# Output projection of a hybrid decoder trunk in three passes instead of two, with new hand-over times

## The chip, the core and the metric

One core of a Trainium2 chip runs the whole program. Its engines each have their own instruction queue and take it strictly in order: TensorE (PE in the profile, with PEld for its weight loads), VectorE (DVE), ScalarE (ACT), GpSimd (POOL) and SyncE (SP), which here only issues DMAs. They wait for each other by semaphores. The metric is the device time of one execution in microseconds (us); less is better.

## The reference, cut to what matters

```python
for l in range(2):                                   # D=1024, 512 tokens
    p = rms_norm(h, attn_norm[l]) @ w_in[l]          # one projection, three groups of columns
    y_a = rwkv7_mixer(p[:, :896], ...)               # 4 heads of 64: 256 columns
    y_b = retention_mixer(p[:, 896:1920], ...)       # 4 heads of 64: 256 columns
    y_c = mla_mixer(p[:, 1920:], ...)                # latent attention, 8 heads of 64: 512 columns
    h = h + concat(y_a, y_b, y_c) @ w_out[l]         # the output projection
    gu = rms_norm(h, ffn_norm[l]) @ w_gate_up[l]
    h = h + (silu(gu[:, :2816]) * gu[:, 2816:]) @ w_down[l]
return rms_norm(h, final_norm)
```

## The kernel before, in words

Activations lie transposed: 128 channels on the partitions, 512 tokens along the free axis. A float32 operand is split into a rounded part `hi` and a remainder `lo`, and each weight tile into `wh` and `wl` (ACT casts `wh`, L410; DVE or POOL subtracts `wl`, L411), so each product takes three matmuls of 128x128 by 128x512: `wh·hi`, `wh·lo`, `wl·hi` (`gemm`). Weight tiles come from DRAM by SP into three buffers `wr` (`fetch`, L394); the first tiles of the feed-forward's down weights come into the single buffer `gg`, which until then holds the RWKV gate that `group_norm` multiplies with (L890). The tile numbers in `POOL_LO` have their `wl` made on POOL.

`mix[0..7]` are the eight blocks of 128 channels of the concatenated mixers: 0 and 1 from RWKV-7 (`group_norm`), 2 and 3 from retention (`retnet`), 4 to 7 from latent attention (`attend`). An attention head is three score tiles in PSUM (`pd<-u,u`, closed by the causal mask `pd<-cmb,idb`), row maxima (DVE, L983), exponentials (ACT, L985), scaling by 1/sum (L218, parts on DVE and on POOL by `EN` keys `x0` to `x3`), ten transposes (`pm<-ident`, L257), copies (L1000) and, for a pair of heads, `attend` (`pm<-u,u` with 64 columns of weights), whose result L304 and L305 split. Score tiles and dense products share four PSUM banks `pd`.

The output projection (from L1297) waits until `mix[0..3]` are all there, then makes for each of the eight output blocks `m` one PSUM tile of four products (12 matmuls) in the order k = 2, 3, 0, 1, and adds it to the residual `h_` (L1309). The residual is loaded from DRAM just before (L1303). A second part takes `mix[4..7]` in the same way (L1328), its first four blocks without `mix[7]` at first.

The order of all instructions is set at build time by `Driver`. Every mixer, head, group norm and the dense chain is a generator; at each `yield` it hands over. The driver always resumes the ready task of the lowest priority number, keeps a clock that only matmuls advance, and holds a task back for the number of us it yielded, `T[l][key]`. The keys `p_...` are priorities. `dense()` has priority 9, the lowest, so its matmuls fill what the others leave. Engines then run that order; nothing is moved at run time.

Of the kernel before, what the change touches and what calls it, by code (L numbers as in the profile page):

```python
# [23 lines left out]
KT = D // P  # L24
# [108 lines left out]
def lay_out(inp):  # L133
# [56 lines left out]
def tile_trunk(ctx: ExitStack, tc: tile.TileContext, a: dict, out: bass.AP, dbg=None):  # L190
    nc = tc.nc
    act, dve, pool, sp = nc.scalar, nc.vector, nc.gpsimd, nc.sync
# [45 lines left out]
    def psd():  # L238
        return pd.tile([P, S], F32, tag="pd", name=nm("pd"))
# [823 lines left out]
    def dense():  # L1063
        hk = lambda k: h_[k // 2][:, k % 2, :]
# [35 lines left out]
        for l in range(L):  # L1100
            st = {"mix": [None] * KT, "rkv": {}, "qa": [], "ka": [], "PT": {}, "heads": 0}
            mix = st["mix"]
# [7 lines left out]
            ps = psd()  # L1110
# [394 lines left out]
```

## Time and profile before

| | |
|---|---|
| three runs | 1312.43 us median (1306.7 to 1313.23) |
| profiled execution | 1308.13 us, of which 1306.3 us are the profile's span |
| mean granted TensorE clock | 0.993 |
| PE / PEld / DVE / ACT / POOL busy | 1266.3 / 1088.7 / 982.6 / 680.7 / 91.8 us |
| first and last L1309 | 250.9 us and 921.3 us from the span's start |

All stretches below are in us from the span's start. The mixers of layer 0 end near 276 us, those of layer 1 near 925 us; the long runs between are the feed-forward. "Idle" of an engine is span less busy time. Matmuls are pipelined and their ends are modelled, so 24 matmuls in a row take less than 24 times the mean of one.

### The profile page before, as it was taken

The numbers are of one execution on the slowest core, as the hardware profiler recorded it, in microseconds if no ns is written. First come the engines' busy times: TensorE is split into PE (matmuls) and PEld (weight loads), VectorE is DVE, ScalarE is ACT, GpSimd is POOL, SyncE is SP. The second block draws the span as 40 slices with busy tenths as digits, with TensorE's granted clock in tenths as the row PEclk, the third lists the DMA queues.
The fourth block names the chain that finished last, engine by engine and source line by source line (L and its number), as shares of the span: only waits on it lengthen the run. The fifth ranks groups of instructions, "written<-read, shape, count | busy, mean of one in ns | idle before, by whom it ended". The sixth has DMA issues, their size and how long they took to land.

```text
span 1306.3 us, 20183 instructions
## 1 busy us (share of the span) xinstructions
PE 1266.3 (97%) x7802; PEld 1088.7 (83%) x7802; DVE 982.6 (75%) x1653; ACT 680.7 (52%) x1271; POOL 91.8 (7%) x79
## 2 busy tenths in 40 slices
PE   7999999899999999999999998989999999999997
PEld 5788787578899999999877887857788999999996
DVE  7797887747987777777668697585579877777774
ACT  7834456735554444445475345474455544444454
POOL 1040112100000000000012300122100000000000
PEclk9999999999999999999999999989999999999999
DMA  7435421223233333333522523141222333222231
GB/s 243 143 91 158 101 70 46 97 65 97 81 113 98 97 99 111 98 97 106 185 89 85 134 85 77 44 141 41 83 96 67 113 99 112 97 98 97 82 113 65
DMA packets 67512, 131.14 MB, mean 100 GB/s; under 512 B 29044, under 2 KB 33940, under 8 KB 67416
## 3 DMA queue, kind: packets, MB, share of 16 engines
q1 hardware_dynamic: 66040, 128.23, 31.3%
q8 instruction: 61, 1.00, 0.3%
q10 hardware_dynamic: 1232, 1.09, 0.2%
q0 software_dynamic: 144, 0.52, 0.1%
q14 instruction: 35, 0.29, 0.1%
HBM read 117.50 MB, written 9.18 MB: 97 GB/s over the span
## 4 chain that ended last, share of the span: by engine, by line
PE 88%; DVE 6%; ACT 3%; DMA 1%; issue 1%; SPq 0%; DVEq 0%; ACTq 0%
PE pd L250 61%; PE pm L250 25%; PE pm L257 2%; DMA wr<-in_wts_dram 1%; DMA u<-in_xT_dram 1%; DVE wl L411 0%; DVE r L729 0%; DVE r L1467 0%; DVE u L1034 0%; ACT wh L410 0%; DVE r L348 0%; DVE u L1024 0%; DVE u L723 0%; DVE u L719 0%; DVE u L1245 0%
## 5 line engine op out<-in xcount | busy, mean ns | idle before, releaser
L250 PE MATMUL pd<-u,wh 128*128 128x256 f32 (+1 forms) x3136 | 757.1, 334 | 10.7 <-ACT wh L410 5.8
L250 PEld LDWEIGHTS pd<-u,wh 128*128 128x128 f32 x3136 | 529.8, 191 | 73.5 <-issue 8.7
L250 PE MATMUL pd<-u,wl 128*128 128x256 f32 (+1 forms) x1568 | 518.6, 331 | 0.7 <-DVE wl L429 0.6
L250 PEld LDWEIGHTS pd<-u,wl 128*128 128x128 f32 x1568 | 298.7, 191 | 29.4 <-POOL wl L411 0.9
L250 PE MATMUL pm<-u,wh 128*128 128x512 f32 (+1 forms) x800 | 212.0, 352 | 0.7 <-DVE u L1034 0.7
L410 ACT CAST wh<-wr 128x1024 fp32r<-128x1024 f32 (+3 forms) x102 | 98.8, 974 | 148.7 <-PE pd L250 95.8
L250 PEld LDWEIGHTS pm<-u,wh 128*128 128x128 f32 x800 | 139.1, 190 | 18.8 <-DVE u L1034 0.9
L250 PE MATMUL pm<-u,wl 128*128 128x512 f32 (+1 forms) x400 | 140.3, 351 | 0.0
L428 ACT CAST wh<-r 128x512 fp32r<-128x512 f32 x144 | 87.4, 618 | 97.6 <-PE pm L250 51.4
L411 DVE TENSOR_TENSOR wl<-wr,wh 128x1024 fp32r<-128x1024 f32 (+3 forms) x88 | 102.6, 1170 | 41.0 <-ACT wh L410 40.7
L428 ACT CAST wh<-wr 128x512 fp32r<-128x512 f32 x108 | 67.0, 620 | 81.0 <-PE pm L250 54.1
L429 DVE TENSOR_TENSOR wl<-r,wh 128x512 fp32r<-128x512 f32 x144 | 97.6, 687 | 7.6 <-ACT wh L428 5.5
L429 DVE TENSOR_TENSOR wl<-wr,wh 128x512 fp32r<-128x512 f32 x108 | 74.3, 689 | 24.5 <-ACT wh L428 22.3
L250 PEld LDWEIGHTS pm<-u,wl 128*128 128x128 f32 x400 | 75.7, 189 | 10.3
L1390 DVE TENSOR_TENSOR u<-u,pm 128x512 f32<-128x512 f32 x64 | 43.6, 684 | 43.5 <-PE pm L250 43.5
L250 PE MATMUL pm<-u,u 32*32 32x32 f32 (+4 forms) x728 | 67.4, 277 | 4.9 <-DVE u L749 2.8
L411 POOL TENSOR_TENSOR wl<-wr,wh 128x1024 fp32r<-128x1024 f32 (+3 forms) x14 | 29.7, 2125 | 594.1 <-ACT wh L410 594.1
L250 PEld LDWEIGHTS pm<-u,u 32*32 32x32 f32 (+3 forms) x728 | 50.4, 157 | 21.9 <-issue 14.5
L410 ACT CAST wh<-gg 128x1024 fp32r<-128x1024 f32 x32 | 33.6, 1050 | 41.5 <-issue 27.4
L439 DVE TENSOR_TENSOR r<-r,wr 128x512 f32<-128x512 f32 x72 | 49.5, 688 | 0.6
L250 PE MATMUL pd<-u,u 96*128 96x128 f32 (+3 forms) x128 | 45.1, 465 | 4.2 <-ACT u L985 3.4
L411 DVE TENSOR_TENSOR wl<-gg,wh 128x1024 fp32r<-128x1024 f32 x32 | 39.1, 1222 | 7.7 <-ACT wh L410 7.7
(272 smaller groups left out, 1563.8 us busy)
## 6 DMA issues: line engine op xcount, KB each, us to landing
wr<-in_wts_dram SPq DMA_DIRECT2D x142, 512.0 KB, 3.6
gg<-in_wts_dram SPq DMA_DIRECT2D x32, 512.0 KB, 3.3
wr<-in_wts_dram SPq DMA_DIRECT2D x22, 384.0 KB, 3.0
u<-in_xT_dram SPq DMA_DIRECT2D x7, 512.0 KB, 6.3
tb<-tab_d SPq DMA_DIRECT2D x8, 256.0 KB, 4.1
r<-r SPq DMA_DIRECT2D x32, 64.0 KB, 2.0
h_d<-u SPq DMA_DIRECT2D x4, 512.0 KB, 2.7
u<-h_d SPq DMA_DIRECT2D x4, 512.0 KB, 6.5
```

The source lines that it names most:

```text
L250: tc.keep_in_program_order(nc.tensor.matmul(o, lhsT, rhs, start=start, stop=stop, skip_group_check=True))
L257: tc.keep_in_program_order(nc.tensor.transpose(o, x, idn))
L410: act.copy(hi[:, z], t[:, z])
L411: (pool if on in POOL_LO else dve).tensor_tensor(lo[:, z], t[:, z], hi[:, z].bitcast(F32), ALU.subtract)
L428: act.copy(hi[:, z], t)
L429: dve.tensor_tensor(lo[:, z], t, hi[:, z].bitcast(F32), ALU.subtract)
L439: E(key).tensor_tensor(o, x, y, ALU.add)
L1390: dve.tensor_tensor(hk(m), hk(m), ps, ALU.add)
```

## The change

The residual is loaded before the projection's first wait. The first part becomes two passes over all eight output blocks: the first waits only for `mix[2]` and `mix[3]` (retention), the second for `mix[0]` and `mix[1]` (RWKV). Each block then has two products (6 matmuls) per PSUM tile and its own add into the residual, so L1309 runs 32 times instead of 16. The weights are laid out to fit; their bytes and the number of matmuls stay. The third pass, over `mix[4..7]`, is as before.

The tables are set anew. In `EN`, `e563` (a subtraction in RWKV of layer 1) goes from POOL to DVE; `e759` (L890, the gate in `group_norm`), `h1` (the remainder of RWKV's low-rank inputs, L314) and `x0` (the 128-column part of the softmax scaling, L218) go from DVE to POOL. `POOL_LO` has 15 tiles instead of 13. In `T`, most values move; the priorities of layer 0 become 3.43 for RWKV (7.42 before), 6.66 for heads (8.88) and 6.0 for `attend` (0), those of layer 1 become 5.43 for RWKV (0), 7.16 for retention (5.86) and 0 for heads (3.43).

```diff
-POOL_LO = (0, 21, 23, 26, 32, 35, 106, 115, 127, 129, 132, 134, 137)
+POOL_LO = (0, 12, 21, 23, 26, 27, 30, 35, 38, 106, 110, 115, 129, 134, 137)
...
-        for k0 in (0, 512):
-            ws += [np.concatenate([kblk(w, b(P * m), slice(k0, k0 + 512)) for m in (2 * i, 2 * i + 1)], 1) for i in range(4)]
+        for k0 in (256, 0):
+            ws += [np.concatenate([kblk(w, b(P * m), slice(k0, k0 + 256)) for m in range(4 * i, 4 * i + 4)], 1) for i in range(2)]
+        ws += [np.concatenate([kblk(w, b(P * m), slice(512, 1024)) for m in (2 * i, 2 * i + 1)], 1) for i in range(4)]
...
-            yield lambda: all(mix[k] is not None for k in range(4))
-            w = wnext()
             h_ = [ua([P, 2, S]) for _ in range(4)]
             h_src = a["xT"] if l == 0 else h_d
             with tc.issue_after(stream["dma"].ins):
                 for i in range(4):
                     sp.dma_start(h_[i], h_src[:, 2 * i : 2 * i + 2, :])
-            for m in range(KT):
-                if m % 2 == 0 and m > 0:
-                    w = wnext()
-                ps = psd()
-                yield from gemm(ps, w, mix, [(4 * (m % 2) + k, k) for k in (2, 3, 0, 1)])
-                dve.tensor_tensor(hk(m), hk(m), ps, ALU.add)
+
+            for k0 in (2, 0):
+                yield lambda: mix[k0] is not None and mix[k0 + 1] is not None
+                for m in range(KT):
+                    if m % 4 == 0:
+                        w = wnext()
+                    ps = psd()
+                    yield from gemm(ps, w, mix, [(2 * (m % 4) + k, k0 + k) for k in range(2)])
+                    dve.tensor_tensor(hk(m), hk(m), ps, ALU.add)
```

PE in layer 0, where the last steps of the RWKV chains (`Sb`, `R`) meet the first heads. Before, no dense product stands here (nor in the 120 matmuls that follow):

```order
L250 MATMUL pm_2170<-u_644,Sb_312_1693 128x128
L257 MATMUL pm_2177<-ident,r_377_2010 128x128
L257 MATMUL pm_2177<-ident,u_2009 128x128 x3
L250 MATMUL pm_2124<-u_955,u_954 128x128
L250 MATMUL pm_2124<-u_748,u_955 128x128
L250 MATMUL pm_2170<-R_427_2169,u_1436 128x128
L250 MATMUL pm_2191<-u_955,u_748 128x128
```

Of the change, the same place (lines are one higher; `wh_1871` and `wl_1872` are the retention pass's first weights):

```order
L251 MATMUL pm_2170<-u_644,Sb_312_1693 128x128
L251 MATMUL pd_2191<-u_1552,wh_1871 128x512 x2
L251 MATMUL pd_2191<-u_1552,wl_1872 128x512
L258 MATMUL pm_2195<-ident,r_377_2010 128x128
L258 MATMUL pm_2195<-ident,u_2009 128x128 x3
L251 MATMUL pm_2124<-u_955,u_954 128x128
L251 MATMUL pm_2124<-u_748,u_955 128x128
L251 MATMUL pm_2170<-R_427_2169,u_1436 128x128
L251 MATMUL pd_2191<-u_1742,wh_1871 128x512 x2
L251 MATMUL pd_2191<-u_1742,wl_1872 128x512
L251 MATMUL pm_2212<-u_955,u_748 128x128
```

The retention pass is strewn in threes among chains and heads. From here to the layer's last `attend` PE now has 111 matmuls of the projection where it had 84: 27 more.

PE in layer 1, after the scores of heads 0 to 2. Before, three matmuls of a query projection, then the third head's second and third score tile, then transposes:

```order
L250 MATMUL pd_8452<-u_8014,wh_8293 128x512 x2
L250 MATMUL pd_8452<-u_8014,wl_8294 128x512
L250 MATMUL pd_8546<-u_8046,u_8376 128x384
...
L250 MATMUL pd_8558<-cmb,idb 128x256
L257 MATMUL pm_8574<-ident,u_8459 128x128
L257 MATMUL pm_8574<-ident,r_1578_8460 128x128
```

Of the change (`wh_8367` and `wl_8368` are the retention pass):

```order
L251 MATMUL pd_8569<-cmb,idb 128x256
L251 MATMUL pd_8468<-u_8030,wh_8309 128x512 x2
L251 MATMUL pd_8468<-u_8030,wl_8310 128x512
L251 MATMUL pd_8602<-u_7846,wh_8367 128x512 x2
L251 MATMUL pd_8602<-u_7846,wl_8368 128x512
L251 MATMUL pd_8602<-u_7985,wh_8367 128x512 x2
L251 MATMUL pd_8602<-u_7985,wl_8368 128x512
...
L258 MATMUL pm_8627<-ident,u_8475 128x128
L258 MATMUL pm_8627<-ident,r_1586_8476 128x128
```

All nine score tiles of heads 0 to 2 now stand first, then 21 dense matmuls in one block, then the transposes. From there on heads follow each other closely: from the second head's scores to the layer's last `attend` PE has 42 dense matmuls where it had 100: 58 fewer. Everything ahead of this place in layer 1 is in the same order on PE, but for one swap of 3 and 21 matmuls.

SP in layer 0, where RWKV's last parts have gone through DRAM (`ro_d`) and the projection's weights (`wr`) begin. Before, the residual (`u<-in_xT_dram`) stands behind `gg`:

```order
L394 DMA wr_2678<-in_wts_dram 128x1024
L394 DMA wr_2722<-in_wts_dram 128x1024
L394 DMA gg_3215<-in_wts_dram 128x1024
L1303 DMA u_2520<-in_xT_dram 128x1024
L1303 DMA u_2521<-in_xT_dram 128x1024
L1303 DMA u_2522<-in_xT_dram 128x1024
L1303 DMA u_2523<-in_xT_dram 128x1024
L394 DMA wr_2768<-in_wts_dram 128x1024
```

Of the change, the same place on SP, where `wr_2608` is the retention pass's first weights:

```order
L395 DMA wr_2608<-in_wts_dram 128x1024
L395 DMA wr_2724<-in_wts_dram 128x1024
L1302 DMA u_2177<-in_xT_dram 128x1024
L1302 DMA u_2178<-in_xT_dram 128x1024
L1302 DMA u_2179<-in_xT_dram 128x1024
L1302 DMA u_2180<-in_xT_dram 128x1024
L395 DMA wr_2772<-in_wts_dram 128x1024
L395 DMA gg_3231<-in_wts_dram 128x1024
```

The four loads of the residual now go ahead of `gg`. In layer 1 they still stand behind `gg`, but no longer behind the `wr` that followed it.

## Rows read from the trace of the kernel before

**Rows 1.** The page, part 1: busy time (share) x instructions of each engine.

```profile
PE 1266.3 (97%) x7802; PEld 1088.7 (83%) x7802; DVE 982.6 (75%) x1653; ACT 680.7 (52%) x1271; POOL 91.8 (7%) x79
```

**Rows 2.** Busy time by 20 us stretches; columns in the first line.

```profile
core 0: us, PE busy (x) PEld busy (x) DVE busy (x) ACT busy (x) POOL busy (x), PEclk, DMA share, GB/s
220.00:240.00 20.00, 17.33 (x97) 10.76 (x97) 14.06 (x37) 18.07 (x44) 6.24 (x5) 1.00 0.00 1
240.00:260.00 20.00, 18.57 (x108) 13.09 (x105) 15.69 (x39) 13.80 (x34) 2.49 (x2) 1.00 0.45 158
320.00:340.00 20.00, 20.00 (x90) 16.57 (x89) 19.89 (x32) 9.08 (x12) 0.00 (x0) 1.00 0.25 79
880.00:900.00 20.00, 20.00 (x108) 14.23 (x107) 12.34 (x35) 10.46 (x31) 3.73 (x3) 1.00 0.22 80
```

**Rows 3.** The two attention stages, each to the layer's last attend; same columns.

```profile
216.70:275.20 58.50, 54.34 (x303) 37.81 (x301) 38.10 (x90) 37.58 (x91) 8.73 (x7) 1.00 0.22 72
852.60:924.30 71.70, 67.21 (x342) 45.85 (x340) 47.95 (x118) 39.53 (x97) 15.23 (x11) 0.95 0.24 80
```

**Rows 4.** VectorE in time: the last split of retention and of RWKV, layer 0.

```profile
178.45 0.69 DVE L305 TENSOR_TENSOR u<-r,u 128x512 fp32r<-128x512 f32 x1
...
246.50 1.31 DVE L305 TENSOR_TENSOR u<-r,u 128x512 fp32r<-128x512 f32 x2
```

**Rows 5.** TensorE in time, layer 0: instructions that PE waited for.

```profile
234.73 0.44 PE L257 MATMUL pm<-ident,u 128*128 128x128 f32 x2 [1.19 <-ACT r L885]
237.91 0.33 PE L257 MATMUL pm<-ident,u 128*128 128x128 f32 x1 [1.05 <-ACT r L885]
239.69 1.72 PE L250 MATMUL pm<-u,u 128*64 128x512 f32 x8 [0.42 <-DVE r L886]
244.08 0.33 PE L257 MATMUL pm<-ident,u 128*128 128x128 f32 x1 [1.43 <-DVE u L218]
```

**Rows 6.** The chain that ended last: start us, us, what; 36 dense matmuls in a row.

```profile
749.92 8.19 PE pd L250 x36
```

**Rows 7.** TensorE in time, layer 1: score tiles that PE waited for.

```profile
854.83 1.10 PE L250 MATMUL pd<-u,u 96*128 96x512 f32 x2 [0.81 <-PE pd L250]
...
861.07 1.65 PE L250 MATMUL pd<-u,u 96*128 96x384 f32 x2 [3.35 <-ACT u L985]
```

**Rows 8.** The chain that ended last, layer 1: what led to those scores.

```profile
858.11 0.81 ACT r L887
...
858.94 1.28 ACT L985
```

**Rows 9.** Busy time after that wait, layer 1; columns as in rows 2.

```profile
861.00:880.00 19.00, 18.61 (x89) 12.07 (x90) 15.27 (x43) 12.73 (x36) 3.71 (x3) 0.83 0.33 111
```

**Rows 10.** SyncE in time: issues of the gate's buffer and of the residual.

```profile
245.56 0.33 SPq L394 DMA_DIRECT2D gg<-in_wts_dram  x1
245.98 1.97 SPq L1303 DMA_DIRECT2D u<-in_xT_dram  x4
...
862.23 0.35 SPq L394 DMA_DIRECT2D gg<-in_wts_dram  x1
```

**Rows 11.** One line's instructions, L1309: duration min/median/max ns, first and last start.

```profile
L1309 DVE TENSOR_TENSOR u<-u,pd x16: 667/686/690, 250.9 to 921.3; 128x512 f32<-128x512 f32 x16
```

**Rows 12.** POOL and DVE in time, and scaling by line (L218, min/median/max ns).

```profile
845.27 1.29 POOL L1280 TENSOR_TENSOR r<-r,r 128x512 f32<-128x512 f32 x1 [0.97 <-DVE r L1278]
...
845.64 2.00 DVE L411 TENSOR_TENSOR wl<-wr,wh 128x1024 fp32r<-128x1024 f32 x1
...
L218 POOL TENSOR_SCALAR u<-u,rs x16: 1238/1244/1247, 208.3 to 907.4; 128x384 f32<-128x384 f32 x16
```

**Rows 13.** VectorE early in layer 0: the instruction that moves by h1.

```profile
44.79 0.68 DVE L314 TENSOR_TENSOR r<-r,r 128x512 fp32r<-128x512 f32 x1
```

**Rows 14.** TensorE early in layer 0: what waited behind it.

```profile
54.78 0.50 PE L250 MATMUL pm<-r,EX 128*128 128x512 f32 x1 [1.61 <-ACT r L651]
```

**Rows 15.** One line's table loads on ScalarE.

```profile
L345 ACT ACT_TABLE_LOAD  x9: 1283/1283/1283, 28.7 to 958.8; - x9
```

More of the change, by code (lines that the diff above doesn't have):

```diff
@@ L36 @@
 TWO_PI = 2.0 * math.pi
-T = [{'tables1': 0, 'norm1': 0, 'p_rwkv': 7.42, 'p_ret': 0.1, 'p_head': 8.88, 'p_tab': 0, 'p_gn': 0.03, 'p_att': 0.0, 'p_kr': 0, 'angles1': 0, 'angles2': 2.63, 'angles3': 1.74, 'angles4': 0, 'angles5': 0, 'rwkv1': 4.34, 'rwkv2': 8.45, 'rwkv3': 0, 'rwkv4': 0, 'rwkv5': 0.0, 'rwkv6': 1.03, 'rwkv7': 0.0, 'rwkv8': 0.34, 'rwkv9': 4.2, 'rwkv10': 3.21, 'rwkv11': 0.76, 'rwkv12': 4.16, 'rwkv13': 2.42, 'rwkv14': 0.0, 'rwkv15': 0.91, 'rwkv16': 0.36, 'rwkv17': 0.74, 'rwkv18': 14.19, 'rwkv19': 2.06, 'rwkv20': 0, 'rwkv21': 0.0, 'chain1': 0.9, 'chain2': 2.38, 'chain3': 0.55, 'group_norm1': 5.69, 'group_norm2': 3.14, 'group_norm3': 4.4, 'retnet1': 5.58, 'retnet2': 0, 'retnet3': 0.74, 'retnet4': 4.98, 'retnet5': 3.23, 'retnet6': 0.0, 'head1': 9.39, 'head2': 0.76, 'head3': 5.1, 'head4': 1.71, 'attend1': 1.77, 'key_rope1': 1.87, 'latent_norm1': 6.26, 'latent_norm2': 3.58, 'latent_norm3': 0.33, 'sums1': 0.0, 'sums2': 3.84, 'sums3': 5.51, 'sums4': 7.06, 'sums5': 5.22, 'sums6': 5.16, 'sums7': 2.65},
-     {'norm1': 0, 'p_rwkv': 0, 'p_ret': 5.86, 'p_head': 3.43, 'p_gn': 2.27, 'p_att': 0, 'p_kr': 2.33, 'rwkv1': 3.59, 'rwkv2': 5.03, 'rwkv3': 0, 'rwkv4': 0, 'rwkv5': 0, 'rwkv6': 3.29, 'rwkv7': 0.0, 'rwkv8': 7.7, 'rwkv9': 1.93, 'rwkv10': 2.94, 'rwkv11': 0.8, 'rwkv12': 3.89, 'rwkv13': 0.02, 'rwkv14': 0, 'rwkv15': 0.43, 'rwkv16': 0.0, 'rwkv17': 0.73, 'rwkv18': 13.88, 'rwkv19': 0, 'rwkv20': 0.42, 'rwkv21': 0, 'chain1': 0.28, 'chain2': 0.96, 'chain3': 0.67, 'group_norm1': 4.53, 'group_norm2': 2.33, 'group_norm3': 19.85, 'retnet1': 2.13, 'retnet2': 4.42, 'retnet3': 0, 'retnet4': 2.48, 'retnet5': 0, 'retnet6': 0.0, 'head1': 5.26, 'head2': 0.12, 'head3': 8.59, 'head4': 0.73, 'attend1': 0, 'key_rope1': 1.53, 'latent_norm1': 3.38, 'latent_norm2': 0.7, 'latent_norm3': 0.52, 'sums1': 2.53, 'sums2': 2.41, 'sums3': 11.53, 'sums4': 0.22, 'sums5': 0, 'sums6': 11.24, 'sums7': 0.72}]
@@ L41 @@
-EN = {'e499': 'd', 'e535': 'd', 'e541': 'd', 'e542': 'd', 'e563': 'p', 'e564': 'p', 'e565': 'd', 'e592': 'd', 'e593': 'd', 'e594': 'd', 'e595': 'd', 'e757': 'd', 'e759': 'd', 'e773': 'p', 'e826': 'd', 'e968': 'p', 'e969': 'd', 'e970': 'd', 'e909': 'd', 'e1037': 'd', 'e1090': 'd', 'e1096': 'p', 'e1097': 'd', 'e1171': 'd', 'e302': 'd', 'e273': 'd', 'c511': 'a', 'c639': 'a', 'c646': 'a', 'c647': 'a', 'c686': 'a', 'c716': 'a', 'c736': 'a', 'c1008': 'a', 'c498': 'd', 'h1': 'd', 'h2': 'd', 'h3': 'p', 'h4': 'p', 'h5': 'd', 'h6': 'd', 's1': 'd', 's2': 'd', 's3': 'd', 's4': 'd', 'z': 'd', 'x0': 'd', 'x1': 'd', 'x2': 'p', 'x3': 'd'}
+T = [{'tables1': 0, 'norm1': 0.0, 'p_rwkv': 3.43, 'p_ret': 0, 'p_head': 6.66, 'p_tab': 2.02, 'p_gn': 0.0, 'p_att': 6.0, 'p_kr': 0.0, 'angles1': 0, 'angles2': 3.74, 'angles3': 0.0, 'angles4': 0.46, 'angles5': 3.39, 'rwkv1': 4.34, 'rwkv2': 8.45, 'rwkv3': 0, 'rwkv4': 0.0, 'rwkv5': 0, 'rwkv6': 1.03, 'rwkv7': 0.0, 'rwkv8': 2.74, 'rwkv9': 5.5, 'rwkv10': 3.21, 'rwkv11': 0.76, 'rwkv12': 4.16, 'rwkv13': 2.42, 'rwkv14': 0, 'rwkv15': 0.82, 'rwkv16': 0.36, 'rwkv17': 0.74, 'rwkv18': 14.33, 'rwkv19': 2.06, 'rwkv20': 0, 'rwkv21': 1.12, 'chain1': 0.9, 'chain2': 2.38, 'chain3': 0.55, 'group_norm1': 5.69, 'group_norm2': 3.14, 'group_norm3': 4.58, 'retnet1': 5.58, 'retnet2': 0, 'retnet3': 0.74, 'retnet4': 4.98, 'retnet5': 3.23, 'retnet6': 0, 'head1': 9.39, 'head2': 0.36, 'head3': 4.91, 'head4': 1.99, 'attend1': 1.77, 'key_rope1': 3.62, 'latent_norm1': 6.26, 'latent_norm2': 3.54, 'latent_norm3': 0.33, 'sums1': 2.61, 'sums2': 2.56, 'sums3': 0, 'sums4': 10.27, 'sums5': 3.42, 'sums6': 6.78, 'sums7': 2.65},
+     {'norm1': 0, 'p_rwkv': 5.43, 'p_ret': 7.16, 'p_head': 0, 'p_gn': 2.8, 'p_att': 0, 'p_kr': 5.54, 'rwkv1': 3.33, 'rwkv2': 5.03, 'rwkv3': 0, 'rwkv4': 0, 'rwkv5': 0, 'rwkv6': 3.29, 'rwkv7': 0, 'rwkv8': 7.7, 'rwkv9': 1.93, 'rwkv10': 2.94, 'rwkv11': 0.81, 'rwkv12': 3.89, 'rwkv13': 0.02, 'rwkv14': 0, 'rwkv15': 0.58, 'rwkv16': 0, 'rwkv17': 0.73, 'rwkv18': 13.88, 'rwkv19': 0.0, 'rwkv20': 0.42, 'rwkv21': 0.0, 'chain1': 0.28, 'chain2': 0.96, 'chain3': 0.69, 'group_norm1': 4.53, 'group_norm2': 2.33, 'group_norm3': 19.85, 'retnet1': 2.13, 'retnet2': 4.32, 'retnet3': 0, 'retnet4': 1.4, 'retnet5': 0.0, 'retnet6': 0, 'head1': 5.26, 'head2': 0.0, 'head3': 8.59, 'head4': 0.13, 'attend1': 0.0, 'key_rope1': 1.56, 'latent_norm1': 3.38, 'latent_norm2': 1.41, 'latent_norm3': 0.52, 'sums1': 2.53, 'sums2': 8.37, 'sums3': 7.02, 'sums4': 0.16, 'sums5': 4.5, 'sums6': 5.56, 'sums7': 1.81}]
@@ new lines @@
+EN = {'e499': 'd', 'e535': 'd', 'e541': 'd', 'e542': 'd', 'e563': 'd', 'e564': 'p', 'e565': 'd', 'e592': 'd', 'e593': 'd', 'e594': 'd', 'e595': 'd', 'e757': 'd', 'e759': 'p', 'e773': 'p', 'e826': 'd', 'e968': 'p', 'e969': 'd', 'e970': 'd', 'e909': 'd', 'e1037': 'd', 'e1090': 'd', 'e1096': 'p', 'e1097': 'd', 'e1171': 'd', 'e302': 'd', 'e273': 'd', 'c511': 'a', 'c639': 'a', 'c646': 'a', 'c647': 'a', 'c686': 'a', 'c716': 'a', 'c736': 'a', 'c1008': 'a', 'c498': 'd', 'h1': 'p', 'h2': 'd', 'h3': 'p', 'h4': 'p', 'h5': 'd', 'h6': 'd', 's1': 'd', 's2': 'd', 's3': 'd', 's4': 'd', 'z': 'd', 'x0': 'p', 'x1': 'd', 'x2': 'p', 'x3': 'd'}
```

## Prediction

> **What bounds the kernel now.** I read the page first: TensorE is busy 97% of the span [rows 1], so a change that leaves its matmuls as they are can win only what PE waits, 1306.3 - 1266.3 = 40 us in all. Next the table by 20 us stretches, to see where: in the feed-forward PE waits almost never, in the mixers' ends it does [rows 2]. So I cut out the two stages from the first heads to the last `attend` [rows 3]: PE idles 58.50 - 54.34 = 4.16 us in layer 0's and 71.70 - 67.21 = 4.49 us in layer 1's, and in the latter the granted clock is 0.95 instead of 1.00, so that 0.05 x 71.7 = 3.6 us of the full clock are lost. These 12.3 us are all that fillers in the two stages could bring by this measure. Then PE in time. In layer 0 the idle time lies at four places, 1.19 + 1.05 + 0.42 + 1.43 = 4.09 us [rows 5], while ScalarE and VectorE work on group norm and softmax; the dense chain has nothing to give, since it waits for RWKV's split at 247 us although retention's was done at 179 us [rows 4]. In layer 1 it is 0.81 + 3.35 us [rows 7]: a score tile waits until the first exponential frees a PSUM bank, and that stands in ScalarE's queue behind a group norm scaling and a table load [rows 8].
>
> **The change, part by part.** Matmuls: the same number and shapes, 0 us. One costs 8.19 / 36 = 0.2275 us in a row [rows 6].
>
> *Layer 0.* 27 more matmuls stand ahead of the last `attend`, 27 x 0.2275 = 6.14 us. If that `attend` comes no later than now, 6.14 us are won; if it comes 6.14 us later, nothing. The stage would have no more to gain than its 4.16 us of idle time, unless waits hide inside "busy". What idles afterwards I take from the nearest rows by VectorE's density: 12.34 us of DVE per 20 with no idle time of PE, 15.69 with 1.43 [rows 2]. DVE's 38.10 us there [rows 3] get about 11 more adds (111/6 against 84/12 before the last `attend`) at 0.686 us [rows 11], 7.5 us, and lose the 128-column scalings and two gate products to POOL. I have no row for the former alone and put all that leaves at 4 us, at most what ten such short instructions at under 0.7 us hold; that leaves 41.6 us over some 61 us, 13.6 per 20. In proportion PE idles (13.6 - 12.34) / 3.35 x 1.43 = 0.54 per 20, 1.6 us in 61. Gain 4.16 - 1.6 = **2.6 us**, between -2.6 and 6.1. The low end is two additional table loads, 2 x 1.283 us [rows 15]: the two group norms no longer run next to each other, so ScalarE goes back and forth once more between reciprocal roots and exponentials. I put them at 0, since ScalarE's 37.58 + 2.57 us over 61 us are less dense than it is now, but they are the cost if they fall between an L885 and its transposes.
>
> *Layer 1.* PE's order up to the nine score tiles is unchanged, and the exponential that frees the first bank stands behind the same chain on DVE and ACT. So the 3.35 us wait should stay, with the low clock after it [rows 9], and the change gains nothing from the rows that look most promising. The 21 matmuls after the tiles take the place of work that PE already had there: in the 19 us after the wait it idles 0.39 us [rows 9]. What follows is bad for the change: 58 fewer matmuls cover the attention, 58 x 0.2275 = 13.2 us. Those come behind the last `attend`, so the stage must shrink from 71.7 to 58.5 us only to break even. Its density for other engines would then be 47.95 / 58.5 x 20 = 16.4 us of DVE per 20, and 13.5 of ACT [rows 3]. Two rows are near: 240 to 260 with 1.43 us idle per 20 at 15.69 and 13.80 [rows 2], and 861 to 880 with 0.41 per 20 at 16.1 and 13.4 [rows 9]. The second is the same stage and nearly without fillers, but at the low clock; so I take a value nearer to it, 0.7 per 20 over the 50 us after the wait, 1.8 us. Idle time becomes 0.81 + 3.35 + 1.8 = 6.0 for 4.49 us: **-1.5 us**, between -13.2 (the stage as long as now) and +8.1 (all idle time and clock back).
>
> *Early in layer 0.* With `h1` on POOL, 0.68 us [rows 13] leaves DVE ahead of the chain that ends in a wait of PE of 1.61 us [rows 14]; the remainder itself is needed later than that chain's next step. Neighbouring instructions on an engine overlap a little, so I take 0.6 of it: **+0.6 us**, at least 0, at most 0.68.
>
> *Residual.* In layer 0 its loads stand behind `gg`, which is free only at 245.56 us; now they stand ahead of it, behind the second weight tile of the pass, and go out before the first adds are due. In layer 1 they still follow `gg` at 862.23 us [rows 10], four issues in about 2 us, and the first add is due near 870 us, after nine score tiles and three quarters of the block. From the layer 0 issue at 245.98 to the first add at 250.9 [rows 10, 11] is 4.9 us with the wait for the data in it, so in layer 1 they land about 862.6 + 4.9 = 867.5. 0 us, but with only some 2 us to spare; a late load would hold DVE and all reductions behind it.
>
> *Sixteen more adds* are 16 x 0.686 = 11 us of DVE [rows 11], counted above where they fall in a stage, and elsewhere covered by dense matmuls. *The other tables*: `e563` on DVE where PE does not wait, the `POOL_LO` tiles converted ahead of use, new times for the feed-forward's sums; 0, within 1 us either way. *POOL* gets eight more short scalings and two gate products per layer; one of 384 columns takes 1.24 us on it, one product of 512 columns 1.29 [rows 12], so at most 8 x 1.24 + 2 x 1.29 = 12.5 us per layer, off PE's path if they are ready in time.
>
> Here two engines get in each other's way: a conversion on DVE that began 0.37 us after a POOL product took 2.00 us [rows 12], about 0.9 us longer than the 1.1 from POOL's end to its own. The Trainium skill ("SBUF — State Buffer", on SBUF's two separate sides) says that VectorE and GpSimd share one port pair as an exclusive lock held for the whole instruction, the loser waiting; the trace agrees at this place. By the rule the offload is no relief in itself: up to 12.5 us of DVE time blocked per layer instead of about 4 saved; the rival C below would then be the likelier.
>
> Sum: 2.6 - 1.5 + 0.6 = 1.7 us by the middles. In layer 0 I think proportion to density is too severe, because a filler that PE can run while it waits also gives DVE and ACT time to come up; I take 4 us there, close to the idle time that is on show, and so 4.0 - 1.5 + 0.6 = **3.1 us**. The profiled execution's 1308.13 us become 1305.0; it is 4.3 us under the median of the three runs, so the median goes from 1312.43 to **1309.3 us**. The three runs spread over 6.5 us, or 0.5%; that is about what a measurement here can tell from no change.
>
> **Rivals.** *A, a small gain or none* (the forecast, 1306 to 1319 us): 0.52. This includes that the new passes do nothing, 1312.4 us: fillers only move waits within a stage.
>
> *B, both stages close*: 4.16 + 4.49 + 3.6 + 0.6 = 12.9 us, **1299.6 us**. For it: each of the four places in rows 5 has a filler near it now. Against: in layer 1 nothing ahead of the 3.35 us wait moves. 0.23.
>
> *B2, PE waits more than its busy time tells.* Weight loads fill 16.57 of 20 us in a dense stretch, and 10.76 + 13.09 = 23.85 of 40 us at layer 0's place [rows 2]: 33.1 - 23.85 = 9.3 us spare instead of the 4.1 us of idle time. The gain would be 9.3 + 0.6 - 1.5 = 8.4 us, **1304.0 us**. Against: score and `attend` matmuls have fewer weight rows or columns, so they load less without waiting. 0.10. The Trainium skill ("Perfetto Trace Analysis", on the most-contended engine) calls busy weight loads the better measure of headroom and matmul busy time a bad one; the trace can't yet tell which holds here.
>
> *C, slower: too little cover in layer 1.* If the stage there shrinks by x us instead of 13.2, the loss is 13.2 - x, against 4.0 + 0.6 = 4.6 us won in layer 0. It decides against the change from x < 8.6, and is over 0.5% from x < 2.1; at x = 0 the time is 1312.43 - 4.6 + 13.2 = **1321 us**. For it: DVE at 16.4 per 20, the POOL scalings above, and `attend` of two pairs back to back. Against: the 0.41 us per 20 in rows 9. 0.15.
>
> **Range and chances.** Faster by over 0.5% are B and B2, 0.33; within, A, 0.52; slower, C, 0.15. From 1299 us (B) to 1318 us (C with two thirds of its price) no more than 2 in 10 is left out.
>
> **What would show it.** Right: the four waits of rows 5 under 2 us together; first L1309 of layer 0 near 220 us, and of layer 1 near 870; the 3.35 us wait still there; layer 1's last `attend` 10 to 13 us earlier. Wrong: score tiles in layer 0 waiting for a bank that a half-done projection tile holds; an L1309 waiting for the residual in layer 1; idle time of PE before transposes near 875 to 910 us over 4 us.

## The result and the profile after

The changed kernel took 1302.92 us (median of 8, 1300.39 to 1307.89), the kernel before 1311.21 us (8 runs): ratio 0.9945, 95% interval 0.9927 to 0.9964, so 7.2 us or 0.55% faster. Two more measurements, each on one chip beside 29 to 35 executions of the kernel before, gave less:

| | changed, us | before, us | ratio (95%) |
|---|---|---|---|
| first | 1302.92 (8) | 1311.21 (8) | 0.9945 (0.9927 to 0.9964) |
| second, after_again | 1307.29 (12) | 1308.91 (35) | 0.9983 (0.9967 to 0.9999) |
| third, after_third | 1304.99 (12) | 1309.78 (29) | 0.9969 (0.9953 to 0.9984) |

The mean of the three ratios is 0.9966, or 4.5 us; each interval lies below 1, and they do not all overlap. The profiled execution of the first took 1300.39 us with a span of 1298.6 us. The page, part 1, answers to [rows 1]:

```profile
PE 1266.0 (97%) x7802; PEld 1089.0 (84%) x7802; DVE 988.0 (76%) x1647; ACT 683.3 (53%) x1273; POOL 114.8 (9%) x101
```

PE's busy time is the same within 0.3 us; what went is waiting. The two stages of [rows 3] again, each from the same place to the end of the layer's last `attend` (busy time by stretch, columns in the first line):

```profile
core 0: us, PE busy (x) PEld busy (x) DVE busy (x) ACT busy (x) POOL busy (x), PEclk, DMA share, GB/s
215.80:278.10 62.30, 61.02 (x330) 42.82 (x329) 41.77 (x91) 40.99 (x93) 17.92 (x16) 1.00 0.15 43
846.80:904.00 57.20, 52.87 (x282) 34.59 (x281) 42.93 (x105) 36.42 (x95) 19.49 (x19) 0.94 0.24 81
```

In layer 0 the stage holds 27 matmuls more (330 against 303) and is 62.3 us long instead of 58.5; PE idles 62.30 - 61.02 = 1.28 us (4.16 before). In layer 1 the stage is 57.2 us long instead of 71.7, but PE idles 4.33 us (4.49 before), and the clock is no better. PE in time in layer 0, the three longest waits there, against the four of [rows 5]:

```profile
233.57 0.30 PE L258 MATMUL pm<-ident,u 128*128 128x128 f32 x1 [0.41 <-ACT r L886]
...
238.61 0.50 PE L251 MATMUL pm<-r,EX 128*128 128x512 f32 x1 [0.56 <-DVE r L315]
...
240.08 0.73 PE L251 MATMUL pd<-u,wh 128*128 128x512 f32 x2 [0.20 <-ACT u L986]
```

1.17 us are left of 4.09. In layer 1 the wait of [rows 7] is still there, with the low clock behind it, and then PE idles no more (PE in time; busy time by stretch):

```profile
848.96 1.10 PE L251 MATMUL pd<-u,u 96*128 96x512 f32 x2 [0.68 <-issue]
...
855.34 1.33 PE L251 MATMUL pd<-u,u 96*128 96x512 f32 x2 [3.65 <-ACT u L986]
```

```profile
856.00:864.00 8.00, 8.00 (x23) 4.42 (x21) 4.92 (x16) 4.22 (x16) 3.90 (x5) 0.57 0.82 281
864.00:875.00 11.00, 11.00 (x63) 8.78 (x62) 9.80 (x21) 6.60 (x15) 2.79 (x2) 1.00 0.30 100
875.00:918.00 43.00, 43.00 (x243) 30.22 (x242) 29.05 (x68) 22.89 (x59) 9.60 (x10) 1.00 0.10 33
```

The adds of the passes, one line's instructions with first and last start, answer to [rows 11]; behind them the first add of layer 1 (DVE in time):

```profile
L1311 DVE TENSOR_TENSOR u<-u,pd x32: 661/687/690, 217.6 to 917.1; 128x512 f32<-128x512 f32 x32
...
868.15 1.88 DVE L1311 TENSOR_TENSOR u<-u,pd 128x512 f32<-128x512 f32 x3
```

To see where the time went in all kernels alike, the start of the same matmul (counted from the first) is taken in two traces; a column is how much longer or shorter the stretch between two of them is than in the trace of the kernel before. The columns are: start of the program; early layer 0 (26 to 57 us before); end of layer 0's mixers (174 to 291); a wait in the feed-forward (354 to 360); begin of layer 1 (659 to 736); its retention and RWKV (776 to 806); its attention (854 to 941); begin of its feed-forward (958 to 1031); last matmul against last matmul.

```text
               start early  L0end  ffn0  L1beg  L1mid  L1att  ffn1   all
after          -0.83 -0.04  -2.46 -1.18  +0.05  -1.34  -1.05  -1.00  -7.8
after_again    -0.57 -0.05  -2.46 -1.14  +0.03  -1.32  +0.62  -0.71  -5.5
after_third    -0.45 +0.99  -2.43 -1.49  +1.13  -1.34  -1.05  -1.24  -5.9
layer0_only    +0.32 +0.63  -1.80 -0.36  +2.63  -0.05  -0.04  -0.05  +1.3
layer1_only    -0.04 +0.85  +0.03 -1.07  +4.40  -1.33  +0.59  -0.61  +2.7
engines_only   -0.53 +1.00  -0.41 -1.20  +4.55  +0.10  -0.42  -0.55  +2.1
passes_only    +0.43 +1.30  +0.23 -0.70  +0.03  +1.77  +0.55  +0.11  +3.7
tables_only    -0.10 +0.83  +3.21 -1.07  +4.48  -1.34  +0.80  +0.09  +6.7
engines_back   -0.72 +1.07  -1.78 -0.74  -0.03  -1.37  -1.04  -0.93  -5.7
lo_back        -0.48 -0.04  -2.05 -0.77  +2.65  -1.36  -1.06  -0.71  -3.8
heads_apart    +0.16 +0.97  -2.46 -1.46  +0.06  +1.56  -0.12  +0.75  -0.9
norm_behind    -0.71 +0.99  -2.46 -1.49  +4.43  -1.33  -0.83  +0.79  -0.6
norm_last      -0.50 +0.42  -2.45 -1.04  +2.81  -1.32  -6.70  -1.19  -7.6
```

Columns that change with the kernel (L0end, L1mid, L1att, ffn1) tell of the edits. `start` is negative in ten of the thirteen profiles and `ffn0` (a weight tile from DRAM that DVE waits for) in all, those with the old tables too: the profiled execution of before had late transfers there. A part of `ffn0` may be the change's all the same: with the new `POOL_LO` it is -1.04 to -1.49, with the old one -0.36 to -1.07. `early` and `L1beg` come and go between executions of one and the same kernel.

### The profile page after: what moved, and what is told of

The parts are those of the page before. It is cut to its first block, busy times and chain, and to the rows that moved or that the text cites. A ratio compares the mean times of both kernels' runs of the same rounds, so it can differ in the third digit from the quotient of the medians.

```text
span 1298.6 us, 20237 instructions
## 1 busy us (share of the span) xinstructions
PE 1266.0 (97%) x7802; PEld 1089.0 (84%) x7802; DVE 988.0 (76%) x1647; ACT 683.3 (53%) x1273; POOL 114.8 (9%) x101
## 4 chain that ended last, share of the span: by engine, by line
PE 89%; DVE 5%; ACT 3%; DMA 1%; issue 1%; SPq 0%; DVEq 0%; ACTq 0%
PE pd L251 61%; PE pm L251 26%; PE pm L258 2%; DMA wr<-in_wts_dram 1%; DVE wl L412 0%; DVE r L730 0%; DVE r L1469 0%; DMA u<-in_xT_dram 0%; DVE wl L430 0%; DVE u L724 0%; DVE u L1025 0%; DVE u L720 0%; DVE u L1246 0%; ACT wh L411 0%; DVE r L440 0%
## 5 line engine op out<-in xcount | busy, mean ns | idle before, releaser
L412 DVE TENSOR_TENSOR wl<-wr,wh 128x1024 fp32r<-128x1024 f32 (+4 forms) x86 | 99.1, 1156 | 42.6 <-ACT wh L411 42.4
L412 POOL TENSOR_TENSOR wl<-wr,wh 128x1024 fp32r<-128x1024 f32 (+4 forms) x16 | 34.8, 2176 | 504.1 <-ACT wh L411 504.1
L251 PE MATMUL pd<-u,u 96*128 96x512 f32 (+3 forms) x128 | 45.2, 467 | 4.3 <-ACT u L986 3.6
```

The lines of the kernel that those rows point to most:

```text
L251: tc.keep_in_program_order(nc.tensor.matmul(o, lhsT, rhs, start=start, stop=stop, skip_group_check=True))
L412: (pool if on in POOL_LO else dve).tensor_tensor(lo[:, z], t[:, z], hi[:, z].bitcast(F32), ALU.subtract)
```

## The experiments

Theory P (place): the gain is made where PE waited and a filler now stands, in layer 0; layer 1's attention does as well without fillers. Its rivals: the moves to GpSimd are what helps (E), the parts help only together (W), and the thinner cover in layer 1, which loses 58 dense matmuls there, costs time (the forecast's step).

**One part alone.** The tables are named here by the kernel that they come from:

```diff
 layer0_only, against the kernel before
-T = [T_before[0], T_before[1]]
+T = [T_changed[0], T_before[1]]
+            if l == 0:
+                for k0 in (2, 0):
...
+            else:
+                yield lambda: all(mix[k] is not None for k in range(4))
...
 layer1_only: the same with T_before[0], T_changed[1] and l == 1
 engines_only
-EN, POOL_LO = EN_before, POOL_LO_before
+EN, POOL_LO = EN_changed, POOL_LO_changed
 passes_only: the edits of dense() and lay_out() for both layers, all tables as before
```

> Three passes, early residual and the new hand-over times in layer 0 alone; layer 1, EN and POOL_LO as before. Theory P (place): the gain comes from retention's pass as filler while RWKV ends in layer 0, so 2.5 us less than before (about 0.2%), the waits of rows 5 under 1.5 us together, and layer 1's stage as before. Theory E (engines): without the moves from VectorE to GpSimd the stage gives nothing, 0 us, because the added adds fill VectorE. Theory W (whole): the 7 us need all parts at once, so 0 to 2 us here.

> Three passes, early residual and the new times in layer 1 alone; layer 0, EN and POOL_LO as before. Theory P: the attention there keeps TensorE full with 58 fewer matmuls between, so no loss, a gain of about 1 us, with the 3.4 us wait for the exponential still there. My prediction's step (cover): a loss of 1.5 us, idle time of TensorE of 1 to 2 us after that wait. Theory E: without the moves to GpSimd VectorE is late and idle time over 3 us appears between the transposes of heads 3 to 7.

> The new EN and POOL_LO in the kernel before; order, passes and times as before. Theory P: 0 us within 1 us; the wait of 1.61 us behind h1 stays, since ScalarE's chain and not VectorE's ends it. My prediction's step: 0.6 us less. Theory E: 3 to 5 us less than before, found where VectorE or the buffers of the weight tiles are waited for. By the lock of VectorE and GpSimd: up to 4 us more.

> Three passes and early residual with every table as before: 132 matmuls of the projection ahead of layer 0's last attend instead of 84, and 135 instead of 102 between the first head and the last attend of layer 1. Theory P: about 2.5 us less in layer 0, and 0 to 1 us more in layer 1, so 1.5 to 2.5 us less than before. Theory W: no gain without the times, since those were found for the three passes. Cover theory: more than the whole change's 7 us, as both stages get more cover than in it.

Beside 35 executions of before (1307.94 us) they took 1307.95 us (ratio 0.9999, 0.9984 to 1.0014), 1308.86 (1.0001, 0.9987 to 1.0016), 1309.09 (1.0006, 0.9994 to 1.0018) and 1309.69 us (1.0014, 1.0002 to 1.0026). No part alone moves the median ratio by more than 0.14%; the intervals still allow gains of 0.8 to 2.1 us for the first three and none for the last. By place the theory stands better for `layer0_only`, which gains 1.80 us in L0end. `passes_only` gains nothing there (+0.23), although it has 132 fillers instead of 111, and that goes against theory P as it was put: the pass alone is not enough. Where fillers stand, waits shrink, but others come (PE in time, layer 0): the heads' transposes now wait, and behind the last `attend` the third pass waits for the split of its result.

```profile
241.75 0.51 PE L251 MATMUL pm<-r,EX 128*128 128x512 f32 x1 [0.67 <-DVE r L315]
...
252.48 0.30 PE L258 MATMUL pm<-ident,u 128*128 128x128 f32 x1 [1.33 <-DVE rs L987]
...
287.54 0.50 PE L251 MATMUL pd<-u,wh 128*128 128x512 f32 x1 [0.74 <-ACT u L305]
```

Over the whole column PE idles 3.60 us against 4.33 before, and its busy time for the same matmuls is 0.95 us longer, which these rows do not explain (busy time by stretch: before, `passes_only`, `tables_only` of the next experiment):

```profile
174.33:291.10 116.77, 112.44 (x644) 87.10 (x644) 75.40 (x173) 64.73 (x166) 18.91 (x13) 1.00 0.23 73
176.19:293.18 116.99, 113.39 (x643) 86.73 (x644) 80.58 (x181) 67.35 (x168) 19.22 (x13) 1.00 0.24 73
174.83:294.81 119.98, 116.00 (x643) 88.72 (x644) 73.71 (x162) 67.24 (x168) 30.63 (x24) 0.97 0.22 71
```

What can hide gains of this size is the clock of the executions: the mean granted clock of those 35 goes from 0.984 (1313.57 us) over 0.990 (nine, 1306.82 to 1309.06) to 0.993 (three, 1306.58 to 1307.99). `layer0_only` had 0.9883 in the mean, the kernel before 0.9899; at 0.989 it took 1306.06 to 1309.50 us (three), before 1308.81 and 1309.17. A straight line of time against clock through all 47 executions, with the kernel as a second term, puts `layer0_only` 1.5 us (± 0.7, 95%) below the kernel before, `engines_only` 0.9 (± 0.6), `layer1_only` 0.5 (± 0.7), and `passes_only` 1.1 (± 0.6) above it. That is an estimate, and it takes for granted that the edits do not move the clock themselves, which is not shown.

**All tables without the passes, and the whole again.**

```diff
 tables_only, against the changed kernel
-            for k0 in (2, 0):
+            yield lambda: all(mix[k] is not None for k in range(4))
...
+                yield from gemm(ps, w, mix, [(4 * (m % 2) + k, k) for k in (2, 3, 0, 1)])
```

> All new tables with the two passes and the late residual of the kernel before; 72 matmuls of the projection stand ahead of layer 0's last attend, 36 in layer 1's attention. Theory P (retention's pass is the filler): layer 0's four waits come back, 4 us of idle time there, so 1 us faster than before at the most. Theory T (the times alone give it): the waits of layer 0 are under 1.5 us without the pass, and it is as fast as the changed kernel.

> The changed kernel once more, beside the kernel before on one chip. Theory F (fixed effect): about 0.45 to 0.55% faster, 6 to 7 us, at the same mean granted clock as the kernel before; the parts alone gave no more than 1 to 1.5 us each, so the rest is gained where parts meet. Theory C (clock): executions of one kernel spread by 8 us along the granted clock, so part of the first 7 us was the clock of those executions, and now it is about 0.35% faster, 4 to 5 us, as at equal clock.

> The changed kernel a third time, for a third chip and beside the two below. If the difference of the two measurements so far (7.2 us and 2.2 us) is the clock of the executions and of the chip, it is 2 to 5 us faster than before, 2.5 to 4.5 us at equal granted clock.

`tables_only` is slower than before, 1313.18 us against 1309.78 (1.0024, 1.0009 to 1.0039), as theory P would have it. Without retention's pass layer 0's end is 3.21 us longer than before. PE idles there as long as before (119.98 - 116.00 = 3.98 us); the same matmuls are busy 3.56 us longer, at a low clock that stands right at these waits (PE in time, and busy time by stretch):

```profile
234.60 0.50 PE L250 MATMUL pm<-r,EX 128*128 128x512 f32 x1 [0.90 <-ACT r L880]
236.09 0.54 PE L250 MATMUL pm<-r,EX 128*128 128x512 f32 x1 [0.98 <-DVE r L314]
241.72 0.33 PE L257 MATMUL pm<-ident,u 128*128 128x128 f32 x1 [1.56 <-POOL u L218]
```

```profile
240.00:248.00 8.00, 6.20 (x30) 2.84 (x29) 6.88 (x16) 7.09 (x14) 3.94 (x4) 0.79 0.01 3
```

So neither passes (+0.23 us in L0end) nor tables (+3.21) gain there, both together do: 2.43 to 2.46 us in each profile that also has the moves to GpSimd. For this place theory W holds of passes and times. My reading, argued and not tested further: the new times put heads and RWKV closer together, and that needs something to run between. The changed kernel again gave 2.2 and 4.1 us. At a mean granted clock of 0.990 to 0.992 it took 1302.25 to 1305.39 us (12 executions of the three measurements, median 1303.2), the kernel before 1305.13 to 1309.77 us (53 executions on the four chips where its clock is listed, median 1307.4): about 4 us, chips mixed. Chip by chip, the line of time against clock gives 2.4 us (± 0.8) in the second measurement and 4.0 (± 0.7) in the third. In the second both kernels had the same mean clock (0.989), so the clock does not explain why it gave less.

**The moves to GpSimd.**

```diff
 engines_back, against the changed kernel
-EN, POOL_LO = EN_changed, POOL_LO_changed
+EN, POOL_LO = EN_before, POOL_LO_before
 lo_back
-POOL_LO = (0, 12, 21, 23, 26, 27, 30, 35, 38, 106, 110, 115, 129, 134, 137)
+POOL_LO = (0, 21, 23, 26, 32, 35, 106, 115, 127, 129, 132, 134, 137)
```

> The changed kernel with EN and POOL_LO as before: three passes, residual and times stay. Theory F: the moves to GpSimd matter only beside the extra adds, so without them 2 to 3 us of the gain go; layer 1's stage, which was 1.0 us shorter in the changed kernel, is 0.6 us longer, as with layer 1 alone. Theory S (sum of parts): 1.5 to 2 us faster than before. Theory N: the engines do nothing, and it is as fast as the changed kernel.

> The changed kernel with POOL_LO alone as before, so EN's moves (the 128-column scalings, the gate, h1, e563) stay. If the moves of the short instructions are what the attention needs, it is as fast as the changed kernel within 1 us; if it is the conversions of weights (two more on GpSimd, others at other places), it is 2 us slower than it, as with both tables back.

On the chip on which the changed kernel took 1307.29 us (0.9983), `engines_back` and `lo_back` took 1307.09 (0.9991, 0.9975 to 1.0006) and 1306.09 us (0.9985, 0.9969 to 1.0001). Theory N: no difference that the runs can tell. By place EN's moves and POOL_LO together are worth 0.67 us in layer 0's end (-1.78 against -2.45), POOL_LO alone 0.40 of it. In layer 1 `engines_back` loses nothing (-1.04), so the +0.59 of `layer1_only`, on which its expectation was built, was no effect of the engines: in the profile of `layer1_only` the low clock lasts on into the dense block (its stretch 872 to 880 has 0.81), and so it does in `after_again` (+0.62), a profile of the changed kernel itself.

**The wait in layer 1.** First, dense matmuls in its place:

```diff
 heads_apart, against the changed kernel
-            yield T[l]["head1"]
+            yield T[l]["head1"] + (0, 6.0, 9.0)[hh] * l
```

> The changed kernel, with heads 1 and 2 of layer 1 due 6 and 9 us later, so that 15 dense matmuls (3.4 us) stand between the score tiles of heads 0 and 1, where TensorE waits 3.65 us for the first exponential. If that wait is only lack of ready work, it shrinks to under 1 us, the low clock behind it goes too, and the time falls by 3 to 6 us. If the dense tiles themselves wait (for VectorE, which still has the group norm to do, to empty the one free bank), the wait only moves to them, and the time stays within 1 us.

1307.27 us, 0.9981 (0.9964 to 0.9998), as the changed kernel. The second of the two expectations holds: the wait goes to the dense matmuls and is longer (PE and DVE in time):

```profile
861.55 1.19 PE L251 MATMUL pd<-u,wh 128*128 128x512 f32 x2 [5.07 <-DVE u L1295]
```

```profile
857.07 0.68 DVE L984 TENSOR_REDUCE nmx<-pd 128x1 f32<-128x512 f32 x1
...
860.03 1.38 DVE L1295 TENSOR_TENSOR u<-pd,fB 64x512 f32<-64x512 f32 x2
```

Three of the four banks hold head 0's scores, and the fourth is emptied by L1295, which stands in VectorE's queue behind group norm (L889) and row maxima (L984). So I took group norm out of the way, on both engines:

```diff
 norm_behind, against the changed kernel
-        dve.tensor_tensor(q, py, rsqrt(q), ALU.mult)
-        act.activation(q, q, AF.Identity, scale=col("rw_gn_w", l, b), bias=col("rw_gn_b", l, b))
+        rs, pin = rsqrt(q), tc.keep_in_program_order if l == 1 else lambda i: i
+        if l == 1:
+            yield lambda: "s0" in st
+        pin(dve.tensor_tensor(q, py, rs, ALU.mult))
+        pin(act.activation(q, q, AF.Identity, scale=col("rw_gn_w", l, b), bias=col("rw_gn_b", l, b)))
...
+            if hh == 0 and 1 in ibs:
+                st["s0"] = True
 norm_last
-            if hh == 0 and 1 in ibs:
+            if hh == 2 and 1 in ibs:
```

In both, `p_gn` of layer 1 is -1, so that group norm goes on at once when head 0 (or 2) is through; `pin` holds an instruction at its place in its engine's order.

> The changed kernel, with the end of layer 1's group norm (two scalings on VectorE and two on ScalarE, and what hangs on them) held behind the softmax of head 0 on both engines; TensorE's order is unchanged. VectorE's queue then reaches the first row maximum 2.0 us earlier and ScalarE's table load comes ahead of the scalings. If VectorE's and ScalarE's queues are what TensorE's 3.65 us wait in layer 1 is made of, it shrinks to 0.5 to 1.5 us and the time falls by 2 to 5 us against the changed kernel, the more the less low clock follows it. If the wait is only handed on (group norm later, so the gate's buffer, the residual and RWKV's pass later), idle time of 2 us or more appears at the adds of L1311's counterpart or ahead of RWKV's pass, and the time stays within 1 us.

> As norm_behind, but the end of layer 1's group norm is held behind the softmax of all three first heads, so that no scaling of it stands between their exponentials; TensorE's order is again that of the changed kernel. If the 2.88 us that norm_behind still waited at head 2 come from the group norm's second scaling in ScalarE's queue, the two waits together fall from 4.0 to 2 us or less, and the time lies 2 to 4 us under the changed kernel, so 0.4 to 0.6% under the kernel before. If VectorE and ScalarE simply need that long for three heads, the waits stay at 3.5 us or more together, and it is as fast as the changed kernel within 1 us. If the group norm is late for RWKV's pass, TensorE waits ahead of that pass (near 885 to 900 us) instead.

`norm_behind`: 1303.98 us, 0.9959 (0.9947 to 0.9971), beside the changed kernel's 0.9969, no difference. The first wait fell from 3.65 to 0.95 us, but PE waits 2.72 us more at the next head (2.88 in the expectation of `norm_last`): the second scaling of group norm on ScalarE, which waits for DVE, now stands between head 1's exponentials (PE in time; ACT in time):

```profile
858.00 1.12 PE L251 MATMUL pd<-u,u 96*128 96x512 f32 x2 [0.95 <-ACT u L989]
865.44 1.65 PE L251 MATMUL pd<-u,u 96*128 96x256 f32 x4 [2.72 <-ACT u L989]
```

```profile
863.77 0.81 ACT L891 ACTIVATE r<-r,PC 128x512 f32<-128x512 f32 x1 [1.47 <-DVE r L890]
...
864.49 0.46 ACT L989 ACTIVATE r<-pd,nmx 128x256 f32<-128x256 f32 x1
```

`norm_last`: 1300.40 us (six executions, 1298.31 to 1301.09) against 1309.70, 0.9925 (0.9905 to 0.9945): faster than the kernel before. The changed kernel did not run on that chip; the interval lies below those of its second and third measurement and overlaps the first (0.9927 to 0.9964), so in the times alone a gain on the changed kernel is likely and not shown. The trace is plainer: one wait of 0.90 us is left of the two, the clock stays whole, and layer 1's attention is 6.70 us shorter than before, 5.65 shorter than in the first profile of the changed kernel. Over all matmuls this profile is no shorter than that one (-7.6 against -7.8), since a longer low clock at the begin of layer 1 (L1beg, +2.81) took some of it back (PE in time; busy time by stretch):

```profile
858.86 1.13 PE L251 MATMUL pd<-u,u 96*128 96x512 f32 x2 [0.90 <-ACT u L989]
```

```profile
858.00:866.00 8.00, 7.13 (x30) 4.46 (x31) 7.38 (x25) 6.75 (x22) 3.97 (x5) 1.00 0.77 295
866.00:874.00 8.00, 8.00 (x44) 6.19 (x43) 7.94 (x15) 5.22 (x12) 3.89 (x4) 1.00 0.20 68
874.00:914.00 40.00, 40.00 (x234) 27.86 (x233) 28.53 (x69) 23.00 (x61) 10.74 (x11) 1.00 0.12 40
```

## Why the prediction was right, and where not

The forecast was 1309.3 us, 3.1 us faster, in a range of 1299 to 1318; the measurement was 1302.92, 7.2 us faster by the ratio, and 4.5 in the mean of three. The range held, and the sign; the sum was too small. By place the three terms of the sum, 4.0 - 1.5 + 0.6 = 3.1 us, came to 2.45 + 1.05 + 0 = 3.5 us; that these are so close is luck, since each of the three was off by 0.6 to 2.6 us, in both directions. The rest came from places that I had put at 0. At 0.55% the first measurement lies where B and B2 had 0.33 together, the mean of the three, 0.34%, in A's class.

**Layer 0, forecast 4.0 us, measured 2.45.** The mechanism is shown: four waits of 4.09 us became three of 1.17, first add at 217.6 us (forecast near 220), and neither the passes nor the tables alone do it. The size by DVE's density, 2.6 us, was right, and so were its parts: the stage took 62.3 us (forecast some 61) with 41.77 us of DVE (41.6) and 1.28 us of idle time of PE (1.6), so 6.14 us of added matmuls cost 62.3 - 58.5 = 3.8 us and won 2.3. Raising it to 4 was the mistake. The two additional table loads, which I had put at 0 and named as the low end, did come, two switches of ScalarE instead of one (ACT in time, before and after), and the gain stands in spite of them:

```profile
234.69 1.28 ACT L345 ACT_TABLE_LOAD   x1
240.50 1.28 ACT L985 ACT_TABLE_LOAD   x1
```

```profile
233.44 1.28 ACT L346 ACT_TABLE_LOAD   x1
237.82 1.28 ACT L986 ACT_TABLE_LOAD   x1
243.49 1.28 ACT L346 ACT_TABLE_LOAD   x1
246.47 1.28 ACT L986 ACT_TABLE_LOAD   x1
```

**Layer 1, forecast 1.5 us lost, measured 1.05 gained (two profiles) or 0.62 lost (one).** Right: the 3.35 us wait stays (3.65) with the low clock behind it, the first add stands at 868.2 us (forecast near 870), and the last `attend` comes earlier than I said: the stage is 14.5 us shorter (57.2 for the 71.7 of [rows 3]), not 10 to 13. The step that failed is "0.7 per 20": from 864 to 918 PE idles 0.00 us. I carried all of DVE's 47.95 us into the shorter stage, but the work that belongs to the dense matmuls left with them, and 42.93 us remained. And density does not tell idle time there: from 864 to 875 DVE works 9.80 of 11 us, 17.8 per 20, and PE never waits. Where the 1.05 us come from, the rows do not show: over this column PE idles as long as before (3.65 against 3.68 us) at the same mean clock (0.96 in both). The difference between the profiles of one kernel is how long the low clock lasts: 0.57 at 856 to 864 us and 1.00 after it in the first, 0.53 and then 0.83 in the second:

```profile
856.00:864.00 8.00, 8.00 (x19) 4.34 (x18) 4.91 (x17) 4.28 (x16) 4.14 (x5) 0.53 0.78 271
864.00:872.00 8.00, 8.00 (x37) 6.52 (x35) 6.26 (x14) 3.12 (x8) 2.79 (x2) 0.83 0.35 123
```

**Early in layer 0, forecast 0.6 us, measured 0.** The wait of 1.61 us is now 0.23 (PE in time; ACT in time), but PE's next instruction is no earlier:

```profile
52.71 1.05 PE L251 MATMUL pm<-r,EX 128*128 128x512 f32 x2
53.99 0.49 PE L251 MATMUL pm<-r,EX 128*128 128x512 f32 x1 [0.23 <-ACT r L652]
```

```profile
53.21 0.72 ACT L652 ACTIVATE r<-u,PC 128x512 fp32r<-128x512 f32 x1
```

This start is 0.79 us ahead of the 54.78 us of [rows 14], and the stretch had begun 0.74 us ahead. The chain ends on ScalarE (L652), which has no idle time there in either trace; taking 0.68 us from DVE was taking it from the wrong engine. What shrank the wait was the clock: the two matmuls ahead of it took 1.05 us in this execution, in which the granted clock was 0.75 from 52 to 56 us. In the second profile of the same kernel the clock was 1.00 there, and the wait is back (PE in time):

```profile
54.12 0.51 PE L251 MATMUL pm<-r,EX 128*128 128x512 f32 x1 [1.62 <-ACT r L652]
```

`engines_only`, with `h1` on POOL, gains nothing there either (+1.00).

**What I put at 0.** The swap of 3 and 21 matmuls in layer 1 is worth 1.33 us in all profiles with the new order (L1mid) but that of `heads_apart`. Three dense matmuls (0.68 us) now stand where PE waited for RWKV's first products (PE in time, before and after):

```profile
797.23 0.24 PE L250 MATMUL pm<-u,u 32*32 32x32 f32 x2 [1.11 <-ACT u L820]
```

```profile
792.58 0.24 PE L251 MATMUL pm<-u,u 32*32 32x32 f32 x2 [0.43 <-ACT u L821]
```

Half of these 0.68 us come back at a later wait (0.32 us before, 0.65 now), so PE's idle time falls by 0.33 us over the column. The rest of the 1.33 us is a low-clock stretch (0.84 from 800 to 808 us before, 1.00 now) which came in each profile of the old order, and with the new one in that of `heads_apart` alone. And the feed-forward's new times for sums, "0, within 1 us", seem to give 0.6 to 1.2 us at layer 1's feed-forward: in seven of the nine profiles that have them with three passes, and in one of the three with the old times (0.55). Together with 2.45 and 1.05 that is 5.4 to 6.0 us, more than the 4.5 of the mean; `start` and `ffn0`, 2.0 us of the first profile's 7.8, are transfers, and but for what `POOL_LO` may do for `ffn0` no part of the change. Why the first measurement is 3 to 5 us above the other two is not settled: its executions of the changed kernel had 0.991 in the mean, the later ones 0.989, but the clock of before is not listed for it.

**The rivals.** B was wrong for this change but right about what is there: `norm_last` took the second stage's 6.7 us by two engines' queues, not by fillers. B2: spare weight-load time promised 9.3 us in layer 0; the stage gave 2.45, nearer to the 4.16 us of idle time of matmuls. What stood against B2 was half right: in that stage the weights of `attend`, 64 columns, load in 136 ns instead of 189, but those of the score tiles, 96 rows, take 190. The Trainium skill ("Perfetto Trace Analysis", on the most-contended engine) names the share of the peak that the matmuls reach and busy weight loads as the measures of headroom, and not the matmuls' busy time; at this place the measurement decides for the matmuls' idle time, and what a still better order could take no run here shows. C did not come: at x = 0 it wanted the stage unchanged, and the stage shrank by 14.5 us. Nor did the lock of VectorE and GpSimd that the Trainium skill states ("SBUF — State Buffer", on SBUF's two separate sides) cost anything that the runs show: with the offload and without it the time is the same (0.9983 and 0.9991). The residual was in time: what VectorE waited for ahead of its 32 adds was TensorE alone.

## What to carry to other kernels

In this case a dense filler paid only at a place where the engine really waited, and only together with the order that puts it there; where the waiting chain ends on ScalarE's or VectorE's queue, look at that queue's order instead. In such a queue look for the instructions that nobody needs yet: here the scalings at the end of a group norm, standing ahead of the softmax, cost 5.65 us by the traces, more than the 2.45 us that the filler in layer 0 won. An engine's density priced layer 0's idle time well and layer 1's badly; before costing a wait by it, follow the one chain that ends the wait.

## What the runs showed of the hardware

The granted clock fell to its half level (1.2 of 2.4 GHz) at places that differ between executions of one kernel, also where PE had not idled: in `after_third` PE is busy through 48 to 56 us and the clock is 0.66 and 0.50 there (busy time by stretch), where the second profile of the same kernel has 1.00 throughout.

```profile
48.00:52.00 4.00, 4.00 (x13) 2.53 (x11) 3.28 (x5) 2.60 (x5) 0.39 (x1) 0.66 0.67 274
52.00:56.00 4.00, 4.00 (x9) 2.40 (x8) 0.64 (x2) 4.00 (x7) 0.00 (x0) 0.50 0.00 0
```

Executions of one kernel spread by 8 us along it (1313.57 us at 0.984, 1305.13 at 0.991). With differences of 2 to 4 us the clock has to be read beside each time.
